# Value products of two heads or two groups issued in turn on the two halves of the array

## The chip, the cores and the metric

The kernel runs on one core of a Trainium2 chip. The metric is device time in microseconds (us), the median of several executions. TensorE (PE in the profile) multiplies, and writes to PSUM. ScalarE (ACT), VectorE (DVE) and GpSimd (POOL) prepare operands and empty PSUM, and SyncE (SP) issues the transfers. Every engine works through its own list in order; semaphores join the lists.

## What is computed

A trunk of two decoder layers on 256 tokens of 1024 channels, in float32. Layer 0 mixes a short convolution with an eight-head causal attention, layer 1 is a sparse attention with 16 heads in 4 groups, and each is followed by a squared-ReLU MLP. The two places that matter here:

```python
# layer 0, eight heads, v of 64 columns
p = jax.nn.softmax(sc, axis=-1).astype(v.dtype)
return jnp.einsum('bhqs,bshd->bqhd', p, v)
...
# layer 1, groups g of 4 heads r; blocks, selected and window branches
o_cmp = jnp.einsum('bgrqn,bngd->bqgrd', p_cmp.astype(vc.dtype), vc)
o_slc = jnp.einsum('bgrqnl,bgqnld->bqgrd', p.astype(vs.dtype), vs)
o_win = jnp.einsum('bgrqs,bsgd->bqgrd', p.astype(vw.dtype), vw)
return (g_blk[:, :, 0, :, :, None] * o_cmp + g_blk[:, :, 1, :, :, None] * o_slc
        + g_blk[:, :, 2, :, :, None] * o_win)
```

With 256 tokens every block is among the selected ones, and the window reaches over all tokens, so that both of the large branches are plain causal attention with keys and values of their own.

## The kernel before

Tokens lie in two tiles of 128 rows (t = 0 and 1). Large products are made of three rounded passes (high times high, low times high, high times low), each one record of TensorE; weights are streamed in by SP, split into a high part by ACT (L177) and a low part by DVE (L178), and multiplied from `acc` tiles. Products with the values are true float32 products: each of them shows as two records in the trace. A value has 64 columns, so such a product fills 64 columns of the array and 64 of the 128 partitions of a PSUM bank.

The order on TensorE is the order of the Python program (a schedule set by hand); a function can be deferred by a number of nanoseconds on a clock that the program itself counts (`tick`, `defer`), and is then issued between other products. The other engines' lists are ordered by the scheduler.

**Layer 0.** `head_qk` makes the scores of one head and its softmax, `head_t` transposes the probabilities into `psb`, and `head_pv` (L519) multiplies them with the values, one head at a time: the products of an even head go to partitions 0 to 63 of the bank `yp`, those of an odd head to partitions 64 to 127. Each head has four records: two of 256 columns, two of 128.

**Layer 1.** The 32 units of work are heads of one token tile: for `gp` 0 and 1, for t 0 and 1, two groups of four heads. Each turn of the loop at L933 issues the scores of a head (`sc`, L865, two buffers), a number of value products (`PVN`), other products out of a list (`fill`, `FILL`: the other values, the queries of the second half, the output projection as far as its operands are ready), and the transposes of the head that was LAG = 5 turns earlier (`head_t`), which ACT or DVE copies into `pt` (two buffers, L889). Between scores and transposes lie the two reductions on DVE (L871), two exponentials on ACT (L873), a reciprocal on DVE, and two scalings on POOL (L878). `unit_pv` queues the value products of a group and token tile when its four heads are transposed: first one product with the compressed values (`ptc`), then those of the even group on partitions 0 to 63, and after them those of the odd group on partitions 64 to 127:

```python
par, nb = g % 2, t + 1
mms = [(None, vcs[:, gp, :], ("ptc", gp, t))] if par == 0 else []
...
self.mm(yps[gp, t][64 * par:64 * par + 64, :], a, b, False, last, 4)
if last and par == 1:
```

When the last of them is done, ACT and DVE split the bank into `xth` and `xtl` (L926, L927), and the output projection of this token tile may take them as operands.

Of the kernel before, what the change touches and what calls it, by code (L numbers as in the profile page):

```python
# [10 lines left out]
F32 = mybir.dt.float32  # L11
F32R = mybir.dt.float32r
AF = mybir.ActivationFunctionType
# [18 lines left out]
# slots of split weights, and of those held ahead of a turn between layers  # L32
WB = 5
XB = 3
# products that wake the tensor engine while the first loads run
WARM = 12
# distances, in the order of the products, between the start of a chain and its use
X_T = (3000.0, 3700.0)
HEAD_EVERY, HEAD_T, HEAD_PV = (3500.0, 3100.0, 1700.0)
# sparse attention: heads between scores and transposes; products with the values per head, and the share  # L40
# of other products beside each head, along the sequence of heads
LAG = 5
PVN = (1, 1, 2, 2, 5, 3)
FILL = (900.0, 1400.0, 650.0, 250.0, 400.0, 1000.0, 450.0, 850.0, 1000.0, 1100.0, 1300.0, 1400.0)


class Pairs:
    """Four column tiles of one token tile, kept in pairs beside those of the other."""
# [9 lines left out]
class Trunk:  # L58
    """Products are issued in the order that this program gives; work whose operands other engines
    prepare is deferred by the time that they take, and issued between the products of the main stream."""  # L60
# [138 lines left out]
    def group_steps(self, x, wname, j, nkt, n, epi, side, k=2, order=(0, 1), cs=None, major="t"):  # L199
        """One column group: all rows of the weight, both token tiles."""  # L200
        if cs is None:
            cs = self.chunks(wname, j, range(nkt // k), k, n)
        ps, begun = {}, set()
        if major == "t":
            seq = [(t, kt) for t in order for kt in range(nkt)]
        else:
            seq = [(t, c * k + i) for c in range(nkt // k) for t in order for i in range(k)]
        if major == "c":
            # the first rows: what needs the low part of the weights comes last
            for kt in range(2):  # L210
                (wh, wl), i = cs[kt // k], kt % k
                for t in order:
                    if t not in ps:
                        ps[t] = self.acc(side)[:, :n]
                    for a in self.xslice(x, t, kt):
                        self.mm(ps[t], a, wh[:, i, :], t not in begun, False)
                        begun.add(t)
                for t in order:
                    self.mm(ps[t], self.xslice(x, t, kt)[0], wl[:, i, :], False, False)
            seq = [(t, kt) for t, kt in seq if kt >= 2]  # L220
        for t, kt in seq:
            if t not in ps:
                ps[t] = self.acc(side)[:, :n]
            self.kstep(ps[t], x, t, kt, cs[kt // k], kt % k, kt == 0, kt == nkt - 1)
            if kt == nkt - 1:
                epi(t, ps[t])
            yield

    def first_two(self, a, b):
        """Two groups after a turn: rows of the second lie between the token tiles of the first."""  # L230
        for _ in range(8):
            next(a)
        for _ in range(2):
            next(b)
        for _ in a:
            pass
        self.close_extra()
        for _ in b:
            pass
# [15 lines left out]
    def transposed(self, src, gcols, res, q, new=None, n=4):  # L255
        """hi/lo of (src * gain)^T for n column tiles, into res[q]."""
        new = new or self.xt_tile
        h, l = new("h"), new("l")
        ps = self.trp()
        for i in range(n):  # L260
            self.tr(ps[:, i, :], src[:, i * P:(i + 1) * P])
        self.split_scaled([(h[:, i, :], l[:, i, :], ps[:, i, :], gcols[:, i:i + 1]) for i in range(n)])
        res[q] = (h, l)

    def xnorm(self, t):
        """1 / rms of the residual, applied where the products leave PSUM."""
# [38 lines left out]
    def two_sided(self, x, wname, nkt, fin, k=2, tail=4, ahead=None):  # L305
        """[256, nkt*128] @ [.., 1024] into four banks; the last rows token tile by token tile."""
# [70 lines left out]
    def mixer_a(self, x, rx, fin):  # L377
        nc, A = self.nc, self.A
        with ExitStack() as st:
# [113 lines left out]
            yps = [None]  # L493
# [19 lines left out]
            def head_t(h, pr):  # L513
# [4 lines left out]
                psb = ap.tile([P, 384], F32, name="psb", tag="psb", bufs=2)  # L518
                nc.vector.tensor_copy(psb.rearrange("p (a b) -> p a b", a=3), ptp[:, 0:3, :])  # L519
                self.defer(HEAD_PV, lambda: head_pv(h, psb))  # L520

            def head_pv(h, psb):
                if h % 2 == 0:
                    yps[0] = pp.tile([P, 512], F32, name="yp", tag="yp", bufs=1)[:, :256]
                y = yps[0]
                o = y[64 * (h % 2):64 * (h % 2) + 64, :]
                self.mm(o, vs[0][:, h, :], psb[:, 0:256], True, False, 4)
                self.mm(o[:, 128:256], vs[1][:, h, :], psb[:, 256:384], False, True, 4)
                if h % 2 == 1:
                    for t in range(2):  # L530
                        mh, ml = mla[t]
                        nc.scalar.activation(mh[:, h // 2, :], y[:, t * P:(t + 1) * P], AF.Copy)
                        nc.vector.tensor_tensor(ml[:, h // 2, :], y[:, t * P:(t + 1) * P],
                                                mh[:, h // 2, :].bitcast(F32), op=OP.subtract)
                if h == A_HEADS - 1:
                    for t in range(2):
                        mixT[t][0] = mla[t]
# [42 lines left out]
    def rope(self, dst, src, tab, h):  # L580
        """dst, src [P, h, 32]; tab [P, 2, 16] holds cos and sin."""
# [22 lines left out]
    def compress(self, pool, pp, z, w1, name, hout):  # L604
        """gelu of the hidden layer over the blocks, transposed: [64, group, block]."""
# [17 lines left out]
    def mixer_c(self, x, rx, fin):  # L623
        nc, A = self.nc, self.A
        with ExitStack() as st:
# [159 lines left out]
            # products that fill the tensor engine's time beside the attention  # L785
# [100 lines left out]
            def head_t_(gp, g, t, r, pb):  # L886
                n = 2 * (t + 1)
                if r == 0:
                    pts[g, t] = qp.tile([P, 4, 4, P], F32, name="pt", tag="pt", bufs=2)[:, 0:n]  # L889
# [9 lines left out]
            def unit_pv(gp, g, t):  # L899
                """Queues the products of a unit with the values."""  # L900
                par, nb = g % 2, t + 1
                mms = [(None, vcs[:, gp, :], ("ptc", gp, t))] if par == 0 else []
                for b in range(2 * nb):
                    br, kb = b // nb, b % nb
                    mms.append((par, vv[kb][:, br * 2 + gp, 64 * par:64 * par + 64],
                                pts[g, t][:, b].rearrange("p a b -> p (a b)")))
                for i, m in enumerate(mms):
                    pvq.append((gp, g, t) + m + (i == len(mms) - 1,))
# [5 lines left out]
            def pv_(n):  # L914
                for _ in range(min(n, len(pvq))):
                    gp, g, t, par, a, b, last = pvq.pop(0)
                    if par is None:
                        yps[gp, t] = self.acc(1)
                        self.mm(yps[gp, t], a, ptc[gp, t], True, False)
                        continue  # L920
                    self.mm(yps[gp, t][64 * par:64 * par + 64, :], a, b, False, last, 4)
                    if last and par == 1:
# [10 lines left out]
            for i in range(len(heads) + LAG + 8):  # L933
# [17 lines left out]
                if 0 <= j < len(heads):  # L951
                    head_t(*heads[j], prob.pop(j))
                    if heads[j][3] == REP - 1:
                        late.append(heads[j][:3])
# [7 lines left out]
    def cmp_scores(self, qp, pp, qT, kc, cbias, gates, gp, t, ptc):  # L962
        """Probabilities of the compressed branch for 8 heads, gate and 1/sum folded in, transposed."""
# [35 lines left out]
    def start(self, x):  # L999
        """Loads x transposed and the first weights, in the order of their use."""  # L1000
# [74 lines left out]
def _rows(w, k, n):  # L1075
    """[K, N] -> [N/n, K/(128k), 128, k*n]: the pieces that the kernel streams, each contiguous."""
# [94 lines left out]
```

## Time and profile before

| what | value |
|---|---|
| median of 3 runs | 661.79 us (661.36 to 661.84) |
| the profiled execution, first to last instruction (span) | 659.7 us |
| around the span, against the median | 2.1 us |
| TensorE busy | 648.9 us, 98% of the span, 3150 records |
| VectorE, ScalarE, GpSimd busy | 418.6, 383.3, 78.8 us |
| chain that ended last, share of TensorE | 96% |

Of the profiled execution no time but its span is recorded; the 2.1 us around it are taken as the same for both kernels. A record's start is exact, its length is modelled: what a product costs is read from the distance between two starts, since products overlap at their ends.

### The profile page before, as it was taken

The page shows a single profiled execution, that of the slowest core. Times are in us where ns is not written, and L with a number is a line of the kernel's source. Part 1 is how long each engine was busy: PE and PEld are TensorE (multiplying, and loading weights), DVE is VectorE, ACT ScalarE, POOL GpSimd, SP SyncE. Part 2 cuts the span into 40 slices and gives each one's busy share as a digit, 9 for nine tenths or more (in the row PEclk, how much of TensorE's full clock was granted, in tenths as well). Part 3 has the DMA queues.
Part 4 walks back from the last instruction along what each step waited for, and adds up shares of the span by engine and source line. Part 5 has one row for each costly group of instructions (what it writes and reads, how often), then busy time and mean ns, then how long its engine had stood idle before and what let it go on. Part 6 is the DMA issues. An engine that isn't in the chain of part 4 may idle for free.

```text
span 659.7 us, 9404 instructions
## 1 busy us (share of the span) xinstructions
PE 648.9 (98%) x3150; PEld 518.0 (79%) x3150; DVE 418.6 (63%) x963; ACT 383.3 (58%) x866; POOL 78.8 (12%) x135
## 2 busy tenths in 40 slices
PE   7999999999999999999999999999999999999995
PEld 4889777888888888888889885665888888888884
DVE  5668697766756654447848776574855665644443
ACT  4886556756646644446737778685854665644431
POOL 1202340020000000000200155451200000000000
PEclk9999999999999999999999999999999999999999
DMA  8856335644564665567615722215336465555521
GB/s 275 288 177 225 97 97 192 216 140 155 187 196 138 199 208 194 191 197 245 207 33 159 259 97 93 65 65 192 128 124 191 139 196 182 194 195 193 197 84 64
DMA packets 32608, 110.04 MB, mean 167 GB/s; under 512 B 4080, under 2 KB 4656, under 8 KB 32560
## 3 DMA queue, kind: packets, MB, share of 16 engines
q1 hardware_dynamic: 32560, 109.44, 50.5%
q8 instruction: 25, 0.41, 0.3%
q14 instruction: 23, 0.19, 0.1%
HBM read 108.38 MB, written 1.05 MB: 166 GB/s over the span
## 4 chain that ended last, share of the span: by engine, by line
PE 96%; DMA 1%; issue 1%; DVE 0%; SPq 0%; POOL 0%; ACT 0%; DVEq 0%; POOLq 0%; ACTq 0%
PE acc L104 82%; PE tr L111 6%; PE sc L104 5%; PE tr L116 1%; DMA raw<-in_a_in 1%; PE yp L104 1%; POOL whi L175 0%; DVE wlo L178 0%; SPq L164 0%; SPq L1018 0%; DVE X L287 0%; ACT sq L278 0%; DVE pst L280 0%; DVEq L1167 0%; POOLq L1167 0%
## 5 line engine op out<-in xcount | busy, mean ns | idle before, releaser
L178 DVE TENSOR_TENSOR wlo<-raw,whi 128x512 fp32r<-128x512 f32 (+3 forms) x368 | 236.3, 680 | 103.6 <-ACT whi L177 99.8
L177 ACT ACTIVATE whi<-raw 128x512 fp32r<-128x512 f32 (+3 forms) x362 | 206.6, 615 | 111.3 <-PE acc L104 107.8
L104 PE MATMUL acc<-whi,xtl 128*128 128x512 f32 (+3 forms) x416 | 162.7, 391 | 0.0
L104 PE MATMUL acc<-whi,xth 128*128 128x512 f32 (+3 forms) x416 | 161.9, 389 | 0.9 <-DVE whi L173 0.9
L104 PE MATMUL acc<-wlo,xth 128*128 128x512 f32 (+3 forms) x416 | 160.1, 386 | 1.8 <-DVE wlo L178 1.8
L104 PE MATMUL acc<-whi,hl 128*128 128x512 f32 x256 | 100.0, 391 | 0.0
L104 PE MATMUL acc<-whi,hh 128*128 128x512 f32 x256 | 99.6, 389 | 0.0
L104 PE MATMUL acc<-wlo,hh 128*128 128x512 f32 x256 | 99.6, 389 | 0.0
L104 PEld LDWEIGHTS acc<-whi,xth 128*128 128x128 f32 x416 | 78.1, 188 | 22.5 <-issue 7.5
L104 PEld LDWEIGHTS acc<-wlo,xth 128*128 128x128 f32 x416 | 77.9, 188 | 18.3 <-DVE wlo L178 3.0
L104 PEld LDWEIGHTS acc<-whi,xtl 128*128 128x128 f32 x416 | 78.1, 188 | 14.6 <-issue 0.2
L104 PEld LDWEIGHTS acc<-wlo,hh 128*128 128x128 f32 x256 | 48.1, 188 | 10.1
L104 PEld LDWEIGHTS acc<-whi,hh 128*128 128x128 f32 x256 | 48.1, 188 | 9.8
L104 PEld LDWEIGHTS acc<-whi,hl 128*128 128x128 f32 x256 | 48.1, 188 | 9.8
L147 POOL TENSOR_TENSOR rp<-mse,mhalf 128x1 f32<-128x1 f32 x8 | 4.4, 550 | 406.3 <-DVE mse L144 406.3
L878 POOL TENSOR_SCALAR pbn<-pbn,sm,gates 128x128 f32<-128x128 f32 (+1 forms) x64 | 39.8, 635 | 81.8 <-DVE sm L875 80.3
L359 ACT ACTIVATE hh<-tr 128x512 fp32r<-128x512 f32 x32 | 19.1, 598 | 49.4 <-PE tr L111 49.4
L360 DVE TENSOR_TENSOR hl<-tr,hh 128x512 fp32r<-128x512 f32 x32 | 22.1, 692 | 40.0 <-ACT hh L359 40.0
L351 DVE TENSOR_TENSOR hs<-hr 128x512 f32<-128x512 f32 x32 | 22.0, 688 | 17.4 <-ACT hr L349 17.4
L349 ACT ACTIVATE hr<-acc,rx 128x512 f32<-128x512 f32 x32 | 22.1, 690 | 18.0 <-PE acc L104 17.4
L873 ACT ACTIVATE pbn<-pbn,nm 128x128 f32<-128x128 f32 (+1 forms) x64 | 28.4, 446 | 4.6 <-DVE nm L871 4.6
L104 PE MATMUL acc<-pt,vv 128*64 128x512 f32 x48 | 23.8, 608 | 0.0
(234 smaller groups left out, 790.1 us busy)
## 6 DMA issues: line engine op xcount, KB each, us to landing
raw<-in_w SPq DMA_DIRECT2D x128, 512.0 KB, 3.4
raw<-in_c_in SPq DMA_DIRECT2D x16, 512.0 KB, 4.0
raw<-in_a_in SPq DMA_DIRECT2D x15, 512.0 KB, 4.6
raw<-in_a_out SPq DMA_DIRECT2D x8, 512.0 KB, 3.9
raw<-in_c_out SPq DMA_DIRECT2D x8, 512.0 KB, 3.4
raw<-in_a_qup SPq DMA_DIRECT2D x6, 384.0 KB, 3.7
gpost<-in_gpost SPq DMA_DIRECT2D x4, 512.0 KB, 4.1
bias<-in_bias SPq DMA_DIRECT2D x4, 512.0 KB, 5.3
```

The costliest lines, as they stand in the source:

```text
L104: self.nc.tensor.matmul(ps, a, b, start=start, stop=stop)
L111: self.nc.tensor.transpose(dst, src, self.ident)
L116: self.nc.tensor.transpose(dst.bitcast(F32R), src, self.ident_r)
L147: nc.gpsimd.tensor_tensor(r, e, self.mhalf, op=OP.pow)
L177: nc.scalar.activation(hi[:, sl], raw[:, sl], AF.Copy)
L178: nc.vector.tensor_tensor(lo[:, sl], raw[:, sl], hi[:, sl].bitcast(F32), op=OP.subtract)
L349: nc.scalar.activation(r, ps, AF.Relu, scale=self.rxof(rx, t))
L351: nc.vector.tensor_tensor(s, r, r, op=OP.mult)
L359: nc.scalar.activation(h, pt, AF.Copy)
L360: nc.vector.tensor_tensor(l, pt, h.bitcast(F32), op=OP.subtract)
L873: nc.scalar.activation(pb[:, sl], pb[:, sl], AF.Exp, bias=nm[:, br:br + 1], scale=-1.0, accum_out=sm[:, br:br + 1])
L878: nc.gpsimd.tensor_scalar(pb[:, sl], pb[:, sl], sm[:, br:br + 1], gates[t][:, 1 + br, h:h + 1], OP.mult, OP.mult)
```

## The change

The value products are no longer queued by group or by head but by pair. In layer 0 `pair_pv` waits for both heads of a pair, and issues the large product of the even head, that of the odd head, then the two small ones. In layer 1 `unit_pv` is called once for two groups, when the odd one is transposed, and every entry of the queue is a pair: for each block of keys the product of the even group, then that of the odd one. `PVN` now counts pairs, and its numbers and those of `FILL` are others; the program's own clock counts two passes for such a product instead of four. `psb` has four buffers instead of two, `pt` three instead of two. (Comments are gone too; lines behind layer 0's pairs are shifted by two, those behind `pv_` by three.)

```diff
-PVN = (1, 1, 2, 2, 5, 3)
-FILL = (900.0, 1400.0, 650.0, 250.0, 400.0, 1000.0, 450.0, 850.0, 1000.0, 1100.0, 1300.0, 1400.0)
+PVN = (1, 1, 1, 1, 3, 3)
+FILL = (900.0, 1400.0, 1200.0, 800.0, 900.0, 1200.0, 900.0, 900.0, 1000.0, 1100.0, 1300.0, 1400.0)
...
-                self.defer(HEAD_PV, lambda: head_pv(h, psb))
-
-            def head_pv(h, psb):
-                if h % 2 == 0:
-                    yps[0] = pp.tile([P, 512], F32, name="yp", tag="yp", bufs=1)[:, :256]
-                y = yps[0]
-                o = y[64 * (h % 2):64 * (h % 2) + 64, :]
-                self.mm(o, vs[0][:, h, :], psb[:, 0:256], True, False, 4)
-                self.mm(o[:, 128:256], vs[1][:, h, :], psb[:, 256:384], False, True, 4)
+                psbs.append(psb)
                 if h % 2 == 1:
...
+                    self.defer(HEAD_PV, lambda: pair_pv(h // 2, [psbs.pop(0), psbs.pop(0)]))
+
+            def pair_pv(p, two):
+
+                y = pp.tile([P, 512], F32, name="yp", tag="yp", bufs=1)[:, :256]
+                o = [y[0:64, :], y[64:128, :]]
+                for i in range(2):
+                    self.mm(o[i], vs[0][:, 2 * p + i, :], two[i][:, 0:256], True, False, 2)
+                for i in range(2):
+                    self.mm(o[i][:, 128:256], vs[1][:, 2 * p + i, :], two[i][:, 256:384], False, True, 2)
...
-                    pts[g, t] = qp.tile([P, 4, 4, P], F32, name="pt", tag="pt", bufs=2)[:, 0:n]
+                    pts[g, t] = qp.tile([P, 4, 4, P], F32, name="pt", tag="pt", bufs=3)[:, 0:n]
...
+                nb = t + 1
+                pvq.append((gp, t, None, False))
                 for b in range(2 * nb):
                     br, kb = b // nb, b % nb
...
+                    pvq.append((gp, t, [(vv[kb][:, br * 2 + gp, 64 * par:64 * par + 64],
+                                         pts[2 * gp + par, t][:, b].rearrange("p a b -> p (a b)"))
+                                        for par in range(2)], b == 2 * nb - 1))
...
-                    self.mm(yps[gp, t][64 * par:64 * par + 64, :], a, b, False, last, 4)
-                    if last and par == 1:
+                    for par, (a, b) in enumerate(pair):
+                        self.mm(yps[gp, t][64 * par:64 * par + 64, :], a, b, False, last, 2)
+                    if last:
...
-                    if heads[j][3] == REP - 1:
-                        late.append(heads[j][:3])
+                    if heads[j][3] == REP - 1 and heads[j][1] % 2 == 1:
+                        late.append((heads[j][0], heads[j][2]))
```

What this does to the lists is shown at three places. On TensorE in layer 0, where the first heads meet their values: before, one head between the products of the main stream (`acc`), its two products in two rows, the second head fifteen rows further on.

```order
L104 MATMUL acc_914<-whi,xth 128x512
L104 MATMUL yp<-psb,vs_92 64x256
L104 MATMUL yp<-psb,vs_93 64x128
L104 MATMUL acc_914<-wlo,xth 128x512
L104 MATMUL sc<-kT,qT 128x128
```

Now both heads stand together (x2), large products first:

```order
L104 MATMUL acc_997<-whi,xth 128x512
L104 MATMUL acc_997<-wlo,xth 128x512
L104 MATMUL yp<-psb,vs_92 64x256 x2
L104 MATMUL yp<-psb,vs_93 64x128 x2
L104 MATMUL sc<-kT,qT 128x128
```

Four such places stand in the new list, eight single ones in the old one. On TensorE in layer 1, at the first heads of the last quarter (`gp` 1, t 1; scores of 512 columns): before, a step of the output projection (`acc_4635`, three rows) lies between the scores of one head and the transposes of another.

```order
L104 MATMUL sc<-kTh,qT 128x512
L104 MATMUL sc<-kTl,qT 128x512
L104 MATMUL acc_4635<-whi,xth 128x512
L104 MATMUL acc_4635<-wlo,xth 128x512
L104 MATMUL acc_4635<-whi,xtl 128x512
L111 MATMUL tr<-ident,pbn 128x128 x2
L104 MATMUL sc<-kTh,qT 128x512
L104 MATMUL sc<-kTl,qT 128x512
```

Now the value pairs of `gp` 0, t 1 end there, and three heads follow each other with no step of the projection between them, since its operands come from that pair's bank (`acc_4563`):

```order
L104 MATMUL acc_4563<-pt,vv_3259 64x512 x2
L111 MATMUL tr<-ident,pbn 128x128 x2
L104 MATMUL sc<-kTh,qT 128x512
L104 MATMUL sc<-kTl,qT 128x512
L111 MATMUL tr<-ident,pbn 128x128 x2
L104 MATMUL sc<-kTh,qT 128x512
L104 MATMUL sc<-kTl,qT 128x512
L111 MATMUL tr<-ident,pbn 128x128 x2
L104 MATMUL sc<-kTh,qT 128x512
L104 MATMUL sc<-kTl,qT 128x512
```

On VectorE at the same place in the new list: the copies of four heads' transposes, the split of the bank (`xtl`) and a part of the compressed branch (`cpc`) stand between the reductions of one head (`nm_4655`) and those of the next (`nm_4678`), whose scores fill one of the two `sc` buffers.

```order
L873 ISA pbn,nm_4655<-sc,bias 128x256
L873 ISA nm_4655 128x1
L897 COPY pt<-tr 128x2x128 x2
L930 TENSOR_TENSOR xtl<-acc_4563,xth 128x512
L897 COPY pt<-tr 128x2x128 x2
L989 TENSOR_TENSOR cpc<-cs_4597,cpc 128x16x16
L877 RECIPROCAL sm_4656<-sm_4656 128x2
L873 ISA pbn,nm_4678<-sc,bias 128x256
L873 ISA nm_4678 128x1
L873 ISA pbn,nm_4678<-sc,bias 128x256
```

In the old list these are spread over a longer stretch of products.

## Rows read from the trace of the kernel before

**Rows 1.** Page: busy time by engine, and the granted clock in 40 slices.
```profile
PE 648.9 (98%) x3150; PEld 518.0 (79%) x3150; DVE 418.6 (63%) x963; ACT 383.3 (58%) x866; POOL 78.8 (12%) x135
...
PEclk9999999999999999999999999999999999999999
```
**Rows 2.** One stretch: length, busy time of PE, PEld, DVE, ACT, POOL, clock, DMA.
```profile
404.00:426.00 22.00, 22.00 (x112) 13.77 (x110) 13.00 (x61) 17.34 (x61) 11.62 (x20) 1.00 0.23 72
```
**Rows 3.** Timeline of TensorE in layer 1: start, length, line, operation, tiles, count.
```profile
429.70 0.40 PE L104 MATMUL acc<-ptc,vcs 128*128 128x512 f32 x1
430.03 1.07 PE L104 MATMUL acc<-pt,vv 128*64 128x512 f32 x2
431.03 0.50 PE L104 MATMUL acc<-whi,xth 128*128 128x512 f32 x1
431.38 0.39 PE L104 MATMUL acc<-wlo,xth 128*128 128x512 f32 x1
431.61 0.39 PE L104 MATMUL acc<-whi,xtl 128*128 128x512 f32 x1
431.83 0.38 PE L111 MATMUL tr<-ident,pbn 128*128 128x128 f32 x2
431.97 0.48 PE L104 MATMUL sc<-kTh,qT 128*128 128x512 f32 x1
...
438.50 1.93 PE L104 MATMUL acc<-pt,vv 128*64 128x512 f32 x4
440.36 0.50 PE L104 MATMUL acc<-whi,xth 128*128 128x512 f32 x1
```
**Rows 4.** Timeline of TensorE in layer 0, around one head's value products.
```profile
73.69 0.40 PE L104 MATMUL acc<-whi,xth 128*128 128x512 f32 x1
74.01 0.86 PE L104 MATMUL yp<-psb,vs 128*64 128x256 f32 x4
74.81 0.50 PE L104 MATMUL acc<-wlo,xth 128*128 128x512 f32 x1
75.15 0.82 PE L104 MATMUL sc<-kT,qT 96*128 96x128 f32 x4
```
**Rows 5.** Timeline of the weight loads in the block of rows 3 that starts at 438.50.
```profile
438.98 0.14 PEld L104 LDWEIGHTS acc<-pt,vv 128*64 128x64 f32 x1 [0.29 <-issue]
439.41 0.14 PEld L104 LDWEIGHTS acc<-pt,vv 128*64 128x64 f32 x1 [0.29 <-issue]
```
**Rows 6.** VectorE and ScalarE by line, 372 to 462 us; mean ns of one.
```profile
L871 DVE CUSTOM_DVE_ANT_0 pbn<-sc,bias 128x256 f32<-128x256 f32 x32 | 12.7, 411 | 1.9 <-issue 1.3 <-PE sc L104 0.4
...
L895 DVE COPY pt<-tr 128x256 f32<-128x256 f32 x16 | 6.7, 422 | 7.2 <-PE tr L111 7.1
L871 DVE DVE_READ_ACCUMULATOR2_ANT nm<- 128x1 f32 x64 | 5.2, 81 | 0.1
L875 DVE RECIPROCAL sm<-sm 128x2 f32<-128x2 f32 x32 | 5.0, 155 | 2.3 <-ACT pbn L873 2.1
...
L927 DVE TENSOR_TENSOR xtl<-acc,xth 128x512 fp32r<-128x512 f32 x4 | 2.8, 689 | 5.7 <-ACT xth L926 5.7
L769 DVE SCALAR_TENSOR_TENSOR q<-acc,rq,q 128x512 fp32r<-128x512 f32 x3 | 2.2, 744 | 0.1
L986 DVE TENSOR_TENSOR cpc<-cs,cpc 128x256 fp32r<-128x256 f32 x4 | 2.2, 540 | 1.6 <-ACT cpc L985 1.6
...
L873 ACT ACTIVATE pbn<-pbn,nm 128x256 f32<-128x256 f32 x32 | 15.9, 498 | 3.3 <-DVE nm L871 3.3
...
L873 ACT ACTIVATE pbn<-pbn,nm 128x128 f32<-128x128 f32 x32 | 12.5, 395 | 1.3 <-DVE nm L871 1.3
L873 ACT ACTIVATION_READ_ACCUMULATOR pbn<-pbn,nm 128x1 f32 x64 | 12.2, 191 | 0.0
L897 ACT ACTIVATE pt<-tr 128x512 f32<-128x512 f32 x16 | 9.4, 589 | 4.3 <-PE tr L111 4.2
...
L768 ACT ACTIVATE q<-acc,rq 128x512 fp32r<-128x512 f32 x3 | 2.1, 690 | 0.9 <-PE acc L104 0.9
```

More of the change, by code (lines that the diff above doesn't have):

```diff
@@ L492, in mixer_a @@
             mla = [[ap.tile([P, 4, P], F32R, name=f"ml{c}{t}") for c in "hl"] for t in range(2)]
-            yps = [None]
+            psbs = []
             def head_qk(h):
@@ L517, in head_t @@
                 self.tr(ptp[:, 2, :], pr[1][:, 128:256])
-                psb = ap.tile([P, 384], F32, name="psb", tag="psb", bufs=2)
+                psb = ap.tile([P, 384], F32, name="psb", tag="psb", bufs=4)
                 nc.vector.tensor_copy(psb.rearrange("p (a b) -> p a b", a=3), ptp[:, 0:3, :])
-                self.defer(HEAD_PV, lambda: head_pv(h, psb))
-            def head_pv(h, psb):
-                if h % 2 == 0:
-                    yps[0] = pp.tile([P, 512], F32, name="yp", tag="yp", bufs=1)[:, :256]
-                y = yps[0]
-                o = y[64 * (h % 2):64 * (h % 2) + 64, :]
-                self.mm(o, vs[0][:, h, :], psb[:, 0:256], True, False, 4)
-                self.mm(o[:, 128:256], vs[1][:, h, :], psb[:, 256:384], False, True, 4)
-                if h % 2 == 1:
[L530 to L535, printed above, removed]
+                psbs.append(psb)
+                if h % 2 == 1:
+                    self.defer(HEAD_PV, lambda: pair_pv(h // 2, [psbs.pop(0), psbs.pop(0)]))
[6 more added lines that the diff above has]
+                    self.mm(o[i][:, 128:256], vs[1][:, 2 * p + i, :], two[i][:, 256:384], False, True, 2)
+                for t in range(2):
+                    mh, ml = mla[t]
+                    nc.scalar.activation(mh[:, p, :], y[:, t * P:(t + 1) * P], AF.Copy)
+                    nc.vector.tensor_tensor(ml[:, p, :], y[:, t * P:(t + 1) * P],
+                                            mh[:, p, :].bitcast(F32), op=OP.subtract)
+                if p == A_HEADS // 2 - 1:
                     for t in range(2):
@@ L897, in head_t_, with unit_pv @@
                     nc.scalar.activation(ph[:, :, r, :], pt[:, 0:n, :], AF.Copy)
-            def unit_pv(gp, g, t):
-                par, nb = g % 2, t + 1
-                mms = [(None, vcs[:, gp, :], ("ptc", gp, t))] if par == 0 else []
+            def unit_pv(gp, t):
+                nb = t + 1
+                pvq.append((gp, t, None, False))
                 for b in range(2 * nb):
                     br, kb = b // nb, b % nb
[L905 to L908, printed above, removed]
+                    pvq.append((gp, t, [(vv[kb][:, br * 2 + gp, 64 * par:64 * par + 64],
+                                         pts[2 * gp + par, t][:, b].rearrange("p a b -> p (a b)"))
+                                        for par in range(2)], b == 2 * nb - 1))
             def pv(*a):
@@ L915, in pv_ @@
                 for _ in range(min(n, len(pvq))):
-                    gp, g, t, par, a, b, last = pvq.pop(0)
-                    if par is None:
+                    gp, t, pair, last = pvq.pop(0)
+                    if pair is None:
                         yps[gp, t] = self.acc(1)
-                        self.mm(yps[gp, t], a, ptc[gp, t], True, False)
+                        self.mm(yps[gp, t], vcs[:, gp, :], ptc[gp, t], True, False)
                         continue
-                    self.mm(yps[gp, t][64 * par:64 * par + 64, :], a, b, False, last, 4)
-                    if last and par == 1:
+                    for par, (a, b) in enumerate(pair):
+                        self.mm(yps[gp, t][64 * par:64 * par + 64, :], a, b, False, last, 2)
+                    if last:
                         mh, ml = self.xt_tile("h"), self.xt_tile("l")
```

## The prediction, made before the changed kernel ran

> **What bounds the kernel now.** I read the page first: TensorE is busy for 98% of the span, at the full level of its granted clock in all 40 slices [rows 1]. The table of stretches says the same of the place of the change: in 404 to 426 us TensorE is busy for the whole 22.0 us, ScalarE for 17.3, VectorE for 13.0, GpSimd for 11.6 [rows 2]. Every microsecond that leaves TensorE's list therefore leaves the span, as long as the other engines keep up. How much room they have is the second question, and the row on ScalarE already says: little. The timeline then gives the price of the value products, and the new list the number and the neighbours of each.
>
> **What a block of value products costs now.** In layer 1 a single product starts 0.33 us behind the record before it, where ordinary records of 512 columns follow each other at 0.23; the next record starts 1.00 us after it; and the one behind that comes at 0.35 instead of 0.23 [rows 3]. A block of two takes 1.86 from its start to the next record, so the second product adds 0.86, which is two records of 0.43. What remains is 0.14 in the block, 0.10 ahead and 0.12 behind it: 0.36 us for entering and leaving the half-array form, whatever the block's size. In the old list 24 products stand in 15 blocks: 24 x 0.86 + 15 x 0.36 = 26.0 us. In layer 0 one head's block takes 0.80 from start to start, with 0.09 more ahead and 0.11 behind [rows 4]: 1.00, of which 0.64 is its four records (0.21, 0.21, 0.11, 0.11 by the 0.43 for 512 columns), and 0.36 again is entry and exit.
>
> **What the new list saves on TensorE.** It has 11 blocks in layer 1: two single products (transposes fall between the two of the first pair), seven pairs by themselves, and twice two pairs. In layer 0 eight blocks become four.
> If the halves do not work side by side, only entries and exits go: 4 x 0.36 = 1.4 us in layer 1, 4 x 0.36 = 1.4 in layer 0, **2.8 us** in all.
> If they do, the order of the list still matters: each product is two records on the same half, so the second waits for the first; only then comes the other half's first record, beside it. n pairs in a row take 2n + 1 record times instead of 4n. Layer 1: 7 x 3 x 0.43 + 2 x 5 x 0.43 + 2 x 0.86 + 11 x 0.36 = 19.0 us, which saves 7.0. Layer 0, a pair: three records of 0.21, then two of 0.11 more, 0.86, and 0.36 for entry and exit: 1.22 against 2.00, times four: 3.1.
> Nothing in the trace of before has two products on different halves in succession, so this term is bounded from both sides: 2.8 us without any overlap, 10.1 with it, and 15.0 if the second half need not wait in the list at all (n pairs in 2n record times: 3.9 us more in layer 1, 0.9 in layer 0). I take the middle one, since weight loads for the next value product already run beside a streaming one here: at 438.98 and 439.41 a load starts with the record before its own [rows 5]. At the change of halves such a load (0.14) may show; over 19 changes that is 0 to 2.7 us, and I take 0.6. **Saved on TensorE: 9.5 us.**
>
> The Trainium skill speaks for the overlap in "TensorEngine Tiling (Array Packing)", Key Properties: tiles in different places of the array load and multiply in parallel. Against it stands "TensorE: Matmul & The Clock Gate", Part 3, The mechanism: weights load beside a running product only where the two use different row groups, and both halves here use all rows. By that rule the other half's weights would come after the product, and the saving would be the 2.8 us. The trace does not bear the rule out: the loads of [rows 5] are on the very rows of the product that streams beside them.
>
> **What comes back as waits.** The new list moves steps of the output projection to the end, and where they stood TensorE now runs from head to head. I followed it engine by engine with the durations of [rows 6], and find waits where before has almost none.
> *The third head of the last quarter* (the places shown for TensorE and VectorE). With two `sc` buffers its scores wait for the reductions of the head two turns back. TensorE gets there in three pairs of transposes (0.14 each) and two pairs of scores (about 0.55 each by the gaps in [rows 3]): 1.5 us. VectorE has to do four copies of 0.42, `xtl` 0.69, `cpc` 0.54, a reciprocal 0.16 and two reductions of 0.41 + 0.08: 4.1 us, and can begin only about 0.1 us behind TensorE. That is 2.7 us of waiting at most; recorded lengths overlap at their ends, and the first copy belongs to transposes ahead of these, so I take **2.0 us**. Queued behind the wait are these scores, the transposes of `cpc` and the first projection steps.
> *The queries of the second token tile.* ScalarE's high part `q` (0.69) now stands in its list behind a copy of `ptc`, two exponentials (0.50 each with 0.19 of readout) and a copy of transposes (0.59), then VectorE's low part (0.74) behind a reduction. From the last product's start that is 0.39 + 1.5 + 0.69 + 0.9 = 3.5 us; TensorE has 2.2 us until it needs their transposes. Wait: **1.3**.
> *The same queries' other tile* and the transpose buffers behind it: 0.2 + 0.7 = **0.9**.
> *Heads 16 to 23.* In this stretch ScalarE is busy 17.3 of 22.0 us before [rows 2]. Its exponentials alone are 8 x 2 x (0.40 + 0.19) = 9.4 us, and eight copies of transposes are 4.7; the new list leaves TensorE about 12 us there. Overlapped starts take back some of the 14, and **0.9** remains, as waits for transpose and `sc` buffers.
> *The turn to the last MLP*: the residual's transposes and the first weights' low parts, **1.4**.
> Together **6.5 us**. The bounds are 0, if TensorE's savings and the scheduler's slack cover them all, and about 9, if the backlog of one place runs on into the next. The third buffer of `pt` and the four of `psb` cost nothing, since no reader is then late; without them the new list's first copies would wait for whole pairs.
>
> **Sum.** 661.8 - 9.5 + 6.5 = **658.8 us**, or 656.7 of span with the 2.1 us around it left as they are.
>
> **Rivals.**
> *The halves run one after the other* (slower). The waits do not lie in the value products, so they come all the same: 661.8 - 2.8 + 6.5 = 665.5 us. For it: no row shows two halves at work, and a float32 product is two records, which may tie up the feeding of the array. Against: the loads of [rows 5]. It decides from a saving below 6.5 us on.
> *The waits stay away*, or the second half need not queue: 661.8 - 9.5 + 3 = 655.3 us with half of the waits, 653.3 with all of the overlap (15.0) and the waits as worked out. For it: before shows no waits of this sort with much the same buffers. Against: ScalarE's 17.3 of 22.0 us [rows 2].
> *The thin stretch costs the clock.* Between 400 and 427 us TensorE would stand still in several places and do mostly transposes. If the granted clock falls to its lower level (1.2 GHz) for some 10 us, about half of them in records that double, 5 us are added: 663.8 us. Against: the clock stays full through all of before [rows 1].
>
> **How the numbers follow.** The forecast has 0.55, with a range of its own of 656.3 to 661.3 (the waits from 4 to 9 us). One after the other: 0.24. Waits stay away or full overlap: 0.14. Clock: 0.07. The range for 8 in 10 is 654.6 to 666.2: below it lies about half of the third case, above it a third of the serial one and a little of the clock case. A measurement of this kernel tells about 0.2%, 1.3 us, from no change. Faster by more than that (below 660.5): 0.42 from the forecast and 0.14 from the third case, 0.56. Slower (above 663.1): 0.24 + 0.05, and 0.01 of the forecast: 0.30. Within: 0.14.
>
> **What would show it.** In the timeline of the changed kernel a lone pair of layer 1 should take about 1.43 us from its first record to the next other record (1.29 + 0.14), against 1.86 if the halves take turns, and 1.00 if they run fully side by side; the other half's first record should start with the first half's second one. In layer 0 the block should take about 1.0 us, not 1.43. TensorE's weight loads should show waits for VectorE and ScalarE of 5 to 8 us in all, the longest near 427 us at the scores, for a reduction on `sc`. The steps of the output projection should end earlier than before by 3 to 4 us. I am wrong in the price of the pair if it takes 1.86, and wrong in the waits if the idle time of TensorE stays below 2 us.

## The result, and the profile after

The changed kernel takes 655.08 us (median of four executions, 653.90 to 657.68), beside 661.61 for the kernel before on the same chip: a ratio of 0.9908, with a 95% interval of 0.9888 to 0.9929. That is 6.5 us faster, where 3.0 were forecast; the time lies inside the range. A second set of executions of the same kernel, taken with the experiments, gave 653.97 us against 661.47, 0.9891 [0.9876, 0.9906]. One execution of a kernel below took 791.06 us at a granted clock of 0.75 throughout; it is left out of that kernel's median.

The page of the changed kernel, busy time and granted clock, beside [rows 1]:

```profile
PE 638.5 (98%) x3150; PEld 515.8 (79%) x3150; DVE 417.7 (64%) x963; ACT 382.8 (59%) x866; POOL 77.8 (12%) x135
...
PEclk9999999999999999999999999989999999999998
```

TensorE has the same 3150 records and is busy for 10.4 us less; the span is 652.9 us, 6.8 less. So 3.6 us went back into idle time, and the clock now falls in one slice of layer 1 (the 8 at the end covers the tail of the span; TensorE's records there still start 0.23 us apart).

**The pairs.** TensorE's timeline in layer 1, a lone pair with what follows it, and a block of two pairs, beside [rows 3]:

```profile
404.95 1.08 PE L104 MATMUL acc<-pt,vv 128*64 128x512 f32 x4
405.96 0.66 PE L111 MATMUL tr<-ident,pbn 128*128 128x128 f32 x4
...
445.45 1.94 PE L104 MATMUL acc<-pt,vv 128*64 128x512 f32 x8
447.32 0.50 PE L104 MATMUL sc<-whi,xth 128*128 128x512 f32 x1
```

A pair, four records, takes 1.01 us to the next start: what one product alone took before (1.00). Two pairs take 1.87, what two products took (1.86). The second half costs 0.01 us. The forecast had said 1.43 for a pair. The weight loads of that lone pair, beside [rows 5], show why:

```profile
404.94 0.20 PEld L104 LDWEIGHTS acc<-pt,vv 128*64 128x64 f32 x4
405.95 0.14 PEld L111 LDWEIGHTS tr<-ident,pbn 128*128 128x128 f32 x1 [0.81 <-issue]
```

All four loads of the pair, two for each half, lie in the first 0.20 us: the odd group's product does not wait until the even group's second record is under way, it starts beside its first. The first records of the two halves start 0.006 us apart.

**Layer 0**, the first two blocks of two heads, beside [rows 4]:

```profile
77.28 0.87 PE L104 MATMUL yp<-psb,vs 128*64 128x256 f32 x8
78.09 0.92 PE L104 MATMUL sc<-kT,qT 96*128 96x128 f32 x4
...
84.92 1.21 PE L104 MATMUL yp<-psb,vs 128*64 128x256 f32 x8
86.06 0.66 PE L111 MATMUL tr<-ident,cu 128*128 128x128 f32 x4
```

Two heads take 0.81 us, as one did (0.80). The second block takes 1.14, because the odd head's `psb` comes 0.34 us late from VectorE; its loads start at 85.26, those of the even head at 84.92:

```profile
85.26 0.62 PEld L104 LDWEIGHTS yp<-psb,vs 128*64 128x64 f32 x6 [0.15 <-DVE psb L519]
```

**The waits.** What TensorE waited for, over the whole span (engine, line, what ended the wait; us in total, times, longest):

```profile
PE sc L104 <- DVE nm L873: 1.7, 1, 1.7
PE tr L116 <- DVE q L771: 1.3, 1, 1.3
PE tr L1011 <- DVE wm L1008: 1.2, 1, 1.2
PE acc L104 <- DVE wlo L178: 1.1, 1, 1.1
PE tr L111 <- DVE X L287: 0.8, 1, 0.8
PE tr L116 <- ACT qT L780: 0.7, 1, 0.7
PE tr L111 <- ACT pt L899: 0.6, 1, 0.6
```

The third and fourth rows belong to the start of the kernel, and before had such waits too (3.9 us, 2.3 here). The other five are new, 5.1 us of idle time, and they stand where the forecast had put them: the scores of the third head of the last quarter (1.7), the queries (1.3 and 0.7), heads 16 to 23 (0.6), the turn to the MLP (0.8). From start to start they cost a little more, since a record's length reaches into the next one's start. The longest of them, and what came behind it:

```profile
423.68 0.38 PE L111 MATMUL tr<-ident,pbn 128*128 128x128 f32 x2
425.74 0.47 PE L104 MATMUL sc<-kTh,qT 128*128 128x512 f32 x1 [1.69 <-DVE nm L873]
...
427.39 0.63 PE L104 MATMUL acc<-whi,xtl 128*128 128x512 f32 x1
427.81 0.63 PE L104 MATMUL acc<-whi,xth 128*128 128x512 f32 x1
...
430.53 0.40 PE L104 MATMUL acc<-ptc,vcs 128*128 128x512 f32 x1
```

The scores start 2.06 us after the transposes, where 0.14 is usual [rows 3]: 1.92 lost. Worked out in the same way the other four are 1.44, 0.88, 0.77 and 0.93: 5.9 us in all. Behind the wait, records of 512 columns start 0.43 us apart in place of 0.23: the lower of the two levels of the clock (1.2 GHz), for 3.7 us; it is the slice with 8 in the page's row. In the second set's profiled execution the same waits stand at the same places, the clock stays full throughout, and the span is 651.7 us. From these scores to the product with `ptc` behind them it takes 3.20 us there and 4.79 here: the fall cost 1.6 us.

With these rows the books nearly close. Layer 1 took 26.0 us for its value products; now two single products at 1.22, seven pairs at 1.01 + 0.22 and two double pairs at 1.87 + 0.22 (0.22 for the gaps ahead and behind, as before) are 15.2: 10.8 saved. Layer 0: 8.0 before, 3 x 1.01 + 1.34 = 4.4 now (0.81 and 1.14 with 0.20 for the gaps): 3.6 saved. Together 14.4, less 5.9 given back, is 8.5. The execution at full clock, with the same 3.9 us of waits at the start as before, was 8.0 us shorter than that of before (659.7 to 651.7); the other 0.5 us is not accounted for.

### The profile page after: what moved, and what is told of

It is laid out like the page before. It is cut to its first block, busy times and chain, and to the rows that moved or that the text cites. A ratio compares the mean times of both kernels' runs of the same rounds, so it can differ in the third digit from the quotient of the medians.

```text
span 652.9 us, 9401 instructions
## 1 busy us (share of the span) xinstructions
PE 638.5 (98%) x3150; PEld 515.8 (79%) x3150; DVE 417.7 (64%) x963; ACT 382.8 (59%) x866; POOL 77.8 (12%) x135
## 4 chain that ended last, share of the span: by engine, by line
PE 93%; DVE 2%; issue 1%; ACT 1%; DMA 1%; SPq 0%; POOL 0%; DVEq 0%; POOLq 0%; ACTq 0%
PE acc L104 80%; PE tr L111 6%; PE sc L104 5%; DMA raw<-in_a_in 1%; PE tr L116 1%; PE yp L104 1%; ACT pbn L875 1%; DVE xlo L178 0%; DVE wlo L178 0%; ACT pt L899 0%; DVE X L287 0%; POOL rp L147 0%; DVE pbn L873 0%; DVE pst L280 0%; ACT whi L177 0%
## 5 line engine op out<-in xcount | busy, mean ns | idle before, releaser
L104 PEld LDWEIGHTS acc<-whi,xtl 128*128 128x128 f32 x416 | 78.6, 189 | 14.4
L880 POOL TENSOR_SCALAR pbn<-pbn,sm,gates 128x128 f32<-128x128 f32 (+1 forms) x64 | 37.3, 593 | 77.3 <-DVE sm L877 74.5
L873 DVE CUSTOM_DVE_ANT_0 pbn<-sc,bias 128x128 f32<-128x128 f32 (+1 forms) x64 | 21.2, 348 | 3.3 <-PE sc L104 3.0
```

The lines of the kernel that those rows point to most:

```text
L104: self.nc.tensor.matmul(ps, a, b, start=start, stop=stop)
L873: nc.vector.tensor_tensor_reduce(pb[:, sl], sp[:, sl], bias[:, r, 256 - nk:], -1.0, BIG, OP.add, OP.min, nm[:, br:br + 1])
L880: nc.gpsimd.tensor_scalar(pb[:, sl], pb[:, sl], sm[:, br:br + 1], gates[t][:, 1 + br, h:h + 1], OP.mult, OP.mult)
```

## The experiments

### Is it the alternation, or the new list?

The change also makes fewer blocks, gives `pt` a third buffer and changes the numbers. The first run keeps all that and puts the two products of each pop on one half:

```diff
-                for b in range(2 * nb):
-                    ...
-                    pvq.append((gp, t, [... for par in range(2)], b == 2 * nb - 1))
+                mms = []
+                for par in range(2):
+                    for b in range(2 * nb):
+                        ...
+                        mms.append((par, vv[...], pts[2 * gp + par, t][...], b == 2 * nb - 1))
+                for i in range(0, len(mms), 2):
+                    pvq.append((gp, t, mms[i:i + 2], i + 2 == len(mms)))
```

> The changed kernel with its numbers, its buffers and as many products in each block, but in layer 1 the two products of a pop stand on the same half: the even group's come first, then the odd group's. Layer 0 is left as changed. Theory 'side by side' (the halves run together from their first record, so the alternation is the gain): a block of two products on one half takes 1.86 us in place of the 1.01 us that a pair takes in the changed kernel; twelve pairs at 0.86 are 10.3, less where a block happens to hold both halves, so 663 to 666 us. Rival 'list' (the gain is from the new list: fewer blocks to enter and leave, a third buffer, other numbers): 654.5 to 657 us, and a block of two keeps about 1.0 us. The waits for DVE and ACT stay 6 to 8 us in sum by either.

Measured: 665.27 us, 1.0045 [1.0026, 1.0064] of before. Its timeline of TensorE at the place of the lone pair above:

```profile
406.93 1.93 PE L104 MATMUL acc<-pt,vv 128*64 128x512 f32 x4
408.79 0.66 PE L111 MATMUL tr<-ident,pbn 128*128 128x128 f32 x4
```

The same four records take 1.86 us when they are on one half. The kernel is 10.2 us slower than the changed one by the medians, 10.0 to 10.9 by the distance of each from the kernel before in its own set. The blocks are 9.4 of it: seven of one pair at 0.85 more, two of two pairs at 1.71 more. (The expectation's twelve pairs count one too many: the two products of the first pair stand apart in both kernels.) The alternation is worth more than the whole gain, and without it the new list costs 3.4 us against before (661.85 in this set). The waits stay, 6.0 us where the changed kernel has 5.1: 2.9 us for `nm` (1.8 of it at the same scores), 1.3, 0.8, 0.8 and 0.2 at the other four. So they belong to the list and not to the faster products.

The two layers apart (layer 0 as changed with layer 1 as before, and the other way round):

> The change in layer 0 alone: eight blocks with two heads each in place of sixteen with one; layer 1 is the kernel before. 'Side by side': a block of two heads takes 0.80 us, as one head's did, so the second head of each pair is free with its entry: 3.7 us saved with nothing given back, 0.35 less if one pair waits for its second head as in the changed kernel: 657.7 to 658.4 us. 'Order held' (the step of the prediction, 2n+1 record times for n pairs): 2.7 saved, 659 us. 'List' (only entries saved): 0.7 to 1.4 saved, 660.3 to 661 us.

> The change in layer 1 alone, with its new numbers; layer 0 is the kernel before. 'Side by side, with waits given back': 11 us of products saved, 6.4 of waits and about 1.5 of clock given back: 3 to 4.6 us net, 657.2 to 658.8 us, with the five waits of the changed kernel at the same places and the granted clock at 0.994. 'Order held': 0.6 saved, 661 us. The two halves of the change should add up to the whole, 6.5 us, within 0.5.

Measured: 657.64 us, 0.9929 [0.9907, 0.9951], for layer 0 alone (four blocks in place of eight, not the eight in place of sixteen of the expectation), 4.2 us less than before, with no wait but those of the start; 658.42 us, 0.9938 [0.9914, 0.9963], for layer 1 alone, 3.4 less, with the five waits of the changed kernel to within 0.1 us. The two add up to 7.6, where the change as a whole measured 6.5 and 7.5. Layer 0 has a quarter of TensorE's saving and half of the gain, because nothing is given back there.

### Are the waits the price of the faster products, or of the numbers?

If VectorE and ScalarE could not follow a shorter stretch, no numbers would help. The fourth run has other numbers for layer 1 and no other edit, found by following the lists engine by engine with the durations of the trace:

```diff
-PVN = (1, 1, 1, 1, 3, 3)
-FILL = (900.0, 1400.0, 1200.0, 800.0, 900.0, 1200.0, 900.0, 900.0, 1000.0, 1100.0, 1300.0, 1400.0)
+PVN = (1, 1, 3, 1, 3, 2)
+FILL = (900.0, 1000.0, 800.0, 500.0, 1400.0, 1050.0, 1200.0, 2500.0, 450.0, 1100.0, 1100.0, 1400.0)
```

> The changed kernel with other numbers for layer 1 only: the products per head (1,1,3,1,3,2) and the share of other products beside each head (900, 1000, 800, 500, 1400, 1050, 1200, 2500, 450, 1100, 1100, 1400), chosen so that the tensor engine has other products where it waited for DVE and ACT. Same instructions in number and kind but for blocks. 'Side by side, waits given back': the 6.4 us of waits fall to about 2, the clock has no thin stretch to fall in: 646 to 649.5 us, granted clock 0.997 or above. Rival 'shortage' (DVE and ACT can't keep up with the shorter stretch, so that the waits move to other places whatever the numbers): 654 to 656 us, with waits of 5 us or more elsewhere.

Measured: 647.78 us, 0.978 [0.9757, 0.9802] of before: 14.1 us faster than before, and the fastest of all kernels here. TensorE's waits in it:

```profile
PE acc L104 <- DVE wlo L178: 2.3, 3, 1.5
PE tr L1011 <- DVE wm L1008: 1.2, 1, 1.2
PE acc L104 <- DVE whi L173: 0.9, 1, 0.9
PE tr L116 <- ACT qT L780: 0.4, 1, 0.4
PE tr L111 <- ACT pt L899: 0.3, 1, 0.3
PE tr L111 <- DVE X L287: 0.3, 1, 0.3
```

The first three are the start. Behind it 1.0 us is left of the 5.1. The waits are not all that the numbers change: the value products now stand in four blocks of one pair and four of two, and none by itself, by the same prices 13.3 us where the changed kernel has 15.2. So of the 6.2 to 7.5 us gained over the changed kernel some 1.9 come from fewer blocks, and the rest, for the most part, from the waits. "Shortage" falls: the other engines can follow, if TensorE has other products where their results are late. Two more runs part the numbers from the alternation: the retuned kernel with the edit of the first run, and the changed kernel with the twelve `FILL` numbers of before.

> The retuned kernel (646.1 us span) with the two products of a pop on one half again, as in the first run: what the alternation alone is worth with numbers that leave few waits. Twelve pairs at 0.86 us are 10.3; in blocks of three pops both halves stand in one block and overlap in part. 'The alternation is worth its products, whatever the numbers': 657 to 659 us, 9.5 to 11 slower than the retuned kernel's 647.8. Rival 'part of the retuned gain came from elsewhere and hides products': less than 8 us slower, under 656 us.

> The changed kernel with the shares of other products (the twelve numbers) of the kernel before; products per head as changed. 'The waits come from the pairs (they become ready only when both groups' probabilities are there, and the stretch is shorter), not from the change's own numbers': 6 to 7 us of waits again, but at other places (near 391, 409, 410 and 422 to 424 us), and 652 to 654.5 us, not slower than the changed kernel. Rival 'the new numbers made the waits': with the old ones below 3 us of waits, 648 to 650.5 us.

Measured: 658.62 us, 0.995 [0.9934, 0.9966], for the first, 10.8 above the retuned kernel. The alternation is worth 10 to 11 us with either set of numbers, and the new numbers without it 3.0 us against before. The second took 653.0 us, 0.9871 [0.985, 0.9892], between the rivals in its waits and as expected in its time. Its waits behind the start:

```profile
PE sc L104 <- DVE csm L984: 1.3, 1, 1.3
...
PE tr L116 <- DVE q L771: 0.9, 1, 0.9
PE tr L111 <- DVE X L287: 0.8, 1, 0.8
PE tr L116 <- ACT qT L780: 0.6, 1, 0.6
PE tr L116 <- DVE cpc L989: 0.3, 1, 0.3
PE tr L116 <- DVE sm L877: 0.2, 1, 0.2
```

They are 4.1 us instead of 5.1, against the 6 to 7 expected: at the queries and the turn to the MLP again, and at other scores and the compressed branch. So neither the change's numbers nor those of before fit a list of pairs; the waits are what an unfitted list costs.

### How far do the halves run on their own?

The forecast's step was that the list's order holds across halves. If only the order of the alternation gave the overlap, a list with all of one half ahead of the other would lose it. Two runs, both with `PVN = (1, 1, 5, 5, 5, 5)`, which makes blocks of four, two and four pairs: one alternating, one half by half, in layer 0 too:

```diff
-                    for par, (a, b) in enumerate(pair):
-                        self.mm(yps[gp, t][64 * par:64 * par + 64, :], a, b, False, last, 2)
+                    ...
+                    for par in range(2):
+                        for _, _, two, end in run:
+                            self.mm(yps[gp, t][64 * par:64 * par + 64, :], *two[par], False, end, 2)
```

> The changed kernel with up to five turns of products per head in layer 1 from the third sixth of the heads on (1,1,5,5,5,5 in place of 1,1,1,1,3,3): three blocks, of four, two and four pairs, in place of eight; order within a block alternating as in the change. A block of n pairs takes 0.86 n + 0.15 us; fewer blocks save entries, and the waits lie differently. 650 to 653 us by any theory; it is the base for the next kernel.

> The kernel with blocks of four, two and four pairs, but within a block first all products of one half, then all of the other (A A A A B B B B); in layer 0 likewise both products of one head, then both of the other. Theory 'independent halves' (a product starts as soon as its own half is free, whatever stands ahead of it for the other): a block of four pairs takes 3.6 us, of two 1.9, of two heads 0.80: same time as the kernel with alternating blocks within 0.5 us. Rival 'the list is gone through in order' (a product can't pass one that waits for its half; only the last product of one half and the first of the other overlap): four pairs 6.0 to 6.4 us, two pairs 2.6 to 2.8, two heads 1.1 to 1.3: 8 to 10 us slower than the alternating one.

Measured: 650.32 us, 0.9832 [0.9817, 0.9846], alternating; 653.97 us, 0.9887 [0.987, 0.9905], half by half. Both theories are wrong, each in a part. The last block of four pairs, first alternating, then half by half:

```profile
443.82 3.65 PE L104 MATMUL acc<-pt,vv 128*64 128x512 f32 x16
447.40 0.50 PE L104 MATMUL acc<-whi,xth 128*128 128x512 f32 x1
```

```profile
446.41 5.42 PE L104 MATMUL acc<-pt,vv 128*64 128x512 f32 x16
451.76 0.50 PE L104 MATMUL acc<-whi,xth 128*128 128x512 f32 x1
```

3.58 and 5.35 us: neither equal nor the 6.0 of a list gone through in order. The block of two pairs takes 1.87 in both, and two heads 0.8 in both. Half by half the second half starts at once behind two products of the first, but late behind four. The weight loads of that block tell when:

```profile
446.41 0.19 PEld L104 LDWEIGHTS acc<-pt,vv 128*64 128x64 f32 x2 [0.36 <-issue]
446.89 0.14 PEld L104 LDWEIGHTS acc<-pt,vv 128*64 128x64 f32 x1 [0.29 <-issue]
447.32 0.14 PEld L104 LDWEIGHTS acc<-pt,vv 128*64 128x64 f32 x1 [0.29 <-issue]
447.75 0.14 PEld L104 LDWEIGHTS acc<-pt,vv 128*64 128x64 f32 x1 [0.29 <-issue]
448.18 0.19 PEld L104 LDWEIGHTS acc<-pt,vv 128*64 128x64 f32 x3 [0.29 <-issue]
448.61 0.19 PEld L104 LDWEIGHTS acc<-pt,vv 128*64 128x64 f32 x2 [0.23 <-issue]
```

One load a record until 447.75; at 448.18, when the fifth record of the first half starts and three are left of its eight, there are three: the second half has begun, 1.77 us late. Two such blocks cost 3.5 us, and the times differ by 3.65. The rule read from this, that a product passes at most three records that wait for the other half, was put to a block of three pairs (six records a half, `PVN` of 4):

> Blocks of three pairs in the order A A A B B B (products per head 1,1,4,4,4,4; two such blocks). The run with four showed the second half's first record start together with the fifth record of the first half (three more of it waiting), and with two at once. Theory 'a product passes at most three records that wait for the other half': here it starts together with the third record of the first half, 0.91 us late, and the block takes 3.6 us from its first record to the next instruction (alternating: 2.73). Rival 'it starts with the third product of the first half, whatever the count': 1.77 us late, 4.4 us.

Its loads:

```profile
416.50 0.19 PEld L104 LDWEIGHTS acc<-pt,vv 128*64 128x64 f32 x2 [0.24 <-issue]
416.99 0.14 PEld L104 LDWEIGHTS acc<-pt,vv 128*64 128x64 f32 x1 [0.29 <-issue]
417.42 0.19 PEld L104 LDWEIGHTS acc<-pt,vv 128*64 128x64 f32 x3 [0.29 <-issue]
```

The second half begins with the third record, at 417.42, 0.92 us late, and the block takes 3.64 us to the next start. In both blocks three records of the first half were waiting when the second half began, and in the block of two pairs, where it began at once, three were waiting too. The kernel's one execution took 654.14 us.

### Does the idle time lower the clock?

In the changed kernel the clock fell soon behind the wait of 1.7 us. The fifth run fills the wait with 18 transposes that nobody reads, and moves nothing:

```diff
+                if (gp, g, t, r) == (1, 3, 0, 3):
+                    for b in range(18):
+                        nc.tensor.transpose(pt[:, 2 + b % 2, :], pb[:, 0:P], self.ident)
```

> The changed kernel with 18 extra transposes (their results go to a part of the tile that nobody reads) issued where the tensor engine waits 1.7 us for DVE in the third quarter of the heads of layer 1; nothing else moves. At 0.09 us each they are 1.6 us of work inside the wait. Theory 'the idle time lowers the clock': the wait shrinks below 0.3 us, the granted clock no longer falls in the slice behind it, the six products behind it come every 0.23 us in place of 0.43, and the kernel is 1.2 to 1.8 us faster than the changed one although it does more: 653.3 to 653.9 us. Rival 'the clock falls for another reason (two halves at once, or the thin stretch as a whole)': the products stay at 0.43 us and the time at 655 us.

> The changed kernel as it is, beside the next one on the same chip: 653.9 to 657.7 us, median about 655, granted clock 0.992 to 0.997.

> The kernel of the first run with 18 extra transposes in the 1.7 us wait again, for a profile at full clock and a comparison on one chip. 'The idle time lowers the clock': wait below 0.3 us, the products behind it every 0.23 us, 1.2 to 1.8 us faster than the changed kernel and with less spread. The first run's median was 1.0 us below the changed kernel's earlier median. 'Another reason': products still at 0.43 us, no difference.

Measured: 654.01 us, 0.9887 [0.9872, 0.9903], in the first run; 653.66 us, 0.9883 [0.9867, 0.99], in the second, whose companion, the changed kernel itself, took 653.97. The wait is filled (timeline of the second run):

```profile
424.19 2.13 PE L898 MATMUL tr<-ident,pbn 128*128 128x128 f32 x18
426.07 0.48 PE L104 MATMUL sc<-kTh,qT 128*128 128x512 f32 x1
```

But the expected 1.2 to 1.8 us did not come: 0.3 between the medians, less than the spread. The executions of the second run lie closer together than the companion's (0.3 us against 1.9), as the theory has it, but one of the first run's took 655.72 us at a granted clock of 0.995. The reason for the missing gain shows in the companion: in its profiled execution the wait is there (1.69 us) and the clock does not fall; the records behind it start 0.23 apart:

```profile
426.14 0.47 PE L104 MATMUL sc<-kTh,qT 128*128 128x512 f32 x1 [1.69 <-DVE nm L873]
...
427.52 0.39 PE L104 MATMUL acc<-whi,xtl 128*128 128x512 f32 x1
427.75 0.40 PE L104 MATMUL acc<-whi,xth 128*128 128x512 f32 x1
...
429.34 0.40 PE L104 MATMUL acc<-ptc,vcs 128*128 128x512 f32 x1
```

So the wait does not always bring the fall. Four profiled executions have a wait of 1.7 or 1.8 us there, those of the changed kernel, its repeat, layer 1 alone and the first run: in three of them the clock fell soon behind it. In the profiles without such a wait (before, layer 0 alone, the retuned kernel, the blocks of four pairs, the filled wait) it did not fall there. That fits the theory, but four profiles do not show a cause, and two facts speak against the length of the wait alone: the retuned kernel with the edit of the first run waits 1.81 us at 11.41 us for `wlo`, and the records behind that start 0.23 apart; and the kernel before, which has no such wait in layer 1, has executions with a granted clock of 0.994 too (663.24 us). What decides between the executions stays open.

## Why the prediction was right in direction and wrong in size

**What bounds the kernel, and the price of a block: right.** TensorE's list decides. The 0.86 for a further product on the same half came out again in the first run (1.86 for two), and two pairs now take what two products took.

**The overlap of the halves: the step that failed.** The term "n pairs in a row take 2n + 1 record times" was taken for 9.5 us after its loads, between the bounds of 2.8 and 15.0. Measured, added up from the starts of the blocks: 14.4, the upper bound less two thirds of a microsecond. I held that a product of the other half has to wait in the list behind the second record of the product ahead of it. The loads at 404.94 show that it does not, and the blocks half by half show how far that reaches: past three waiting records. No place in the changed kernel has more of them, so it gets the whole overlap. That every engine works through its own list in order, as stated at the outset, therefore does not hold for TensorE between the halves. The allowance of 0.6 for loads at a change of halves was unneeded too; a pair costs 0.01 more than one product. (Its 19 changes are those from the even to the odd half; with the six back they are 25.) The profile of before could not settle this, as no row of it has two halves in succession; but then the forecast should have given the upper bound, with its time of 653.3 us, more than a share of 0.14.

The Trainium skill was weighed at this step. The Trainium skill's "TensorEngine Tiling (Array Packing)", Key Properties, says that tiles load and multiply in parallel, and the four loads in 0.20 us agree. The Trainium skill's "TensorE: Matmul & The Clock Gate", Part 3, The mechanism, says that loads run beside a product only on other row groups, and that matmuls start and end in the program's order. The traces differ on both, and they decide: both halves use all 128 rows and load beside each other, and in the block half by half the first record of a product that stands later in the list starts at 448.18, with three records of earlier products still to come.

**The waits: right in places and sum.** Forecast 6.5 us in five places, measured 5.9 in these five (1.92, 1.44, 0.88, 0.77, 0.93 against 2.0, 1.3, 0.9, 0.9, 1.4). Four of the five are within 0.15 us. The 2.0 among them was set below a worked-out 2.7, so its nearness is in part luck. What I did not see is that they are no price of the faster products: the first run has them without the alternation, and the retuned kernel is nearly without them.

**The rivals.** "One after the other" is out: a pair takes 1.01 us, not 1.86. The first run makes layer 1 that rival, and its 665.27 us lies close to the 665.5, partly by chance, since it keeps layer 0 in pairs and has a stretch at the lower clock (records 0.43 to 0.56 us apart behind its wait of 1.8). "Full overlap, with the waits as worked out", 653.3 us, is what happened, and the two sets of executions (655.08 and 653.97) lie 1.8 and 0.7 above it. The clock rival came true in some executions at a third of its price: 1.6 us, for 3.7 us at the lower level instead of 10.

**The sum.** 661.8 - 14.4 + 5.9 gives 653.3; with the 0.5 us not accounted for, and nothing to 1.6 for the clock, that is 653.8 to 655.4, and the two sets measured 653.97 and 655.08. The error of 3.7 us is 4.9 of the overlap and 0.6 of the waits, less the 1.8 that the clock and the rest took.

## What to carry to other kernels

When two products use different halves of the array, look for the second half's weight load in the trace: if it lies beside the first half's, the second product is nearly free, and a list needs no strict alternation as long as few records of one half (here three) wait ahead of the other. When a change takes work from the bounding engine, price the waits and the saving apart, since the saving stays while the waits may go with new numbers in the schedule: here 6.5 us became 14.1, some 1.9 of it by fewer blocks. And where a mechanism is bounded from both sides with no row between, the middle is a guess like the ends.

## What the runs showed of the hardware that was not expected

- A float32 product on the other half starts 0.01 us or less behind the one on the first half, though its weights use all rows: four loads in 0.20 us, a pair in 1.01 us, one product in 1.00.
- A product overtakes earlier ones that wait for the other half: it began with three records still waiting there, in blocks of three and of four pairs (0.92 and 1.77 us late), and at once behind two products, whose other three records were waiting (1.87 us for two pairs in either order). No run here tests when the signal of the last product in a list comes if an earlier one ends after it.
- The clock fell to its lower level behind a wait of 1.7 or 1.8 us in three profiled executions of four, for 3 to 4 us, and not in the fourth, nor behind a wait of 1.81 us at the start of another kernel.
